# A modulation vector computed on VectorE in two batches instead of on GpSimd and ScalarE in one

## The chip, the cores and the metric

The kernel runs on one core of a Trainium2 chip. The metric is the device time of one execution in microseconds. Three executions of the kernel before took 1995.58, 1997.78 and 2001.44 us; the median is 1997.78 us.

## The reference, cut to what matters

Two transformer blocks are applied one after the other to 512 tokens of 1024 features, all in float32. Block 1 is a mixer (an mLSTM branch and a sparse attention branch, "NSA", joined and projected by `w_out`) followed by a norm. Block 2 has three sublayers: a SwiGLU feed-forward net (FFN1), a token mixer with a delta rule, and a second feed-forward net (FFN2). Before each sublayer the normed values are shifted and scaled, and each sublayer's result is gated, by vectors that depend on a second input `c` alone:

```python
mod = (jax.nn.silu(c) @ ada_w[l] + ada_b[l]).reshape(B, N_SUBLAYERS, 3, D_MODEL)
shift, scale, gate = mod[:, :, 0], mod[:, :, 1], mod[:, :, 2]
h = modulate(rms_norm(x, norm_g[l, 0]), shift[:, 0], scale[:, 0])
x = x + 0.5 * gate[:, 0, None, :] * swiglu(h, ffn1_w_in[l], ffn1_w_out[l])
```

`ada_w` is 1024 x 9216 (37.7 MB). Its product with one vector is the modulation: nine parts of 1024 values (shift, scale and gate of three sublayers), which the kernel holds as 72 columns of 128. The change is about where and when these 72 columns are computed. FFN1 needs columns 0 to 15 for its norm and 16 to 23 for its gate, the mixer needs 24 to 47, FFN2 needs 48 to 71. Nothing in block 1's values depends on them.

## The kernel before

**The large products.** A plan is a list of groups (`Group`); each group is a product of 512 tokens with up to 1024 x 128 (or x 256, 264, 288, 512) weights. `run` walks the plan. For each piece of 128 x 1024 weights it emits a load into one of three `wr` buffers (line 302), a split into two float32r parts, `wh` on ScalarE and `wl` as a difference on VectorE (two pieces ahead of the product that uses them), and 24 matrix products of 512 columns into a `pg` bank of PSUM (four banks). When a group is full, its bank is read by ScalarE or VectorE ("evacuated").

**The side work.** After each group and in its middle `run` calls `side_step`, which advances the generators in `self.side` (mLSTM, NSA, norms, delta rule) and in `self.bg`. A generator that waits for a flag yields "w".

**The order of the instructions.** The program is emitted in that order, but the framework reorders each engine's instructions by priority (what was emitted earlier goes first) and by its own estimate of when operands and buffers are free. An instruction that was emitted late but whose operands are ready early can therefore stand much earlier in its engine's queue. Each queue is fixed in the built program, and on the chip an engine goes through it strictly in order.

**The modulation before** (`ada`, line 629 on). A generator in `self.bg` starts once block 1's norm is done. It takes 144 half columns: a load of 128 x 512 weights (`adaw`, line 646) into a slot of the common pool, a product with silu(c) (tile `sc`) by GpSimd (`tt` with `eng=nc.gpsimd`, line 220), and a copy by ScalarE that sums each row into one value of `adap` (`accum_out`, line 217, which makes a second instruction on ScalarE, the read of the accumulator). Two loads are in flight. At the end 72 pairs are added and the scale, shift and gate tiles are made. `ada_done`, ahead of the projection by `w_out` (`w_o1`), drains `self.bg`.

**What else the names mean.** `pg` is a bank of a large product, `hh`/`hl` and `uh`/`ul` are split values, `wh`/`wl` split weights; `cx`, `ca`, `ct`, `mqk` are the steps of the convolution that follows the `w_q` and `w_k` groups (line 613 on: two ScalarE reads of the bank, three VectorE steps `ca`, a tanh `ct`, a product `mqk`); `mrow`, `gcol`, `mS` and `mE` belong to the mLSTM; `cs`, `csx`, `cpt`, `sS`, `smx`, `sP`, `src`, `sPT` to NSA (`sP` are the exponentials that GpSimd scales by `src`). `sd` and `su` are two 128 x 1024 tiles of a pool `solve` with one buffer each; the compression of NSA's keys uses them as `kk`, and block 2's delta rule uses them later.

Of the kernel before, what the change touches and what calls it, by code (L numbers as in the profile page):

```python
# [18 lines left out]
P = 128  # L19
# [9 lines left out]
GS = 2                  # heads whose triangles are solved together  # L29
SOLVE_STEP = 4          # columns of them between two products  # L30
SOLVE_DELAY = 7         # steps until the solved ones are back from memory
NV = 2                  # groups of values, of gates, that start before a norm
# [63 lines left out]
def prep(a):  # L96
    """Lays the inputs out for the loads: name -> array."""
# [60 lines left out]
class Group:  # L158
    """One group of a large product: pieces of weights, and what to do with them."""
# [9 lines left out]
class Call:  # L169
    """A place in the plan where something else is put into the program."""  # L170
# [6 lines left out]
class Builder:  # L177
# [56 lines left out]
    def trr(self, out, in_):  # L234
        """transpose of values that float32r holds"""
        return self.nc.tensor.transpose(out.bitcast(F32R), in_, self.identr)
# [9 lines left out]
    def pow(self, out, in_, n):  # L246
        """out = in ** -0.5"""
        self.nc.gpsimd.tensor_tensor(out, in_, self.mhalf[:, 0:n], OP.pow)
# [34 lines left out]
    def later(self, f, *a):  # L283
        """evacuate now, or when the norm that the values lack is there"""
        if self.hold is None:
            with self.tc.high_priority(offset=0):
                f(*a)
        else:
            self.hold.append((f, a))
# [6 lines left out]
    def load(self, upto):  # L296
        """starts the loads of the weights, up to a piece"""
# [8 lines left out]
    def part(self, upto):  # L306
        """splits weights into the two parts that the products take"""
# [15 lines left out]
    def run(self, plan, ahead_dma=3, ahead_split=2):  # L323
# [5 lines left out]
        for g in plan:  # L329
# [6 lines left out]
            for k0, n in g.pieces:  # L336
# [4 lines left out]
                if g.early:  # L341
                    # whole tiles of tokens, one after another: the first in banks of the side work
# [35 lines left out]
                elif g.halves:  # L378
                    if k0 == 0:
                        ps = [self.pg.tile([P, 512], F32, tag="g", name="pg") for _ in range(2)]  # L380
                    if g.mid and k0 + n == g.kts:
                        # the first half of the tokens is done before the second
# [66 lines left out]
    def copies(self):  # L449
        """of the constants, in other types"""  # L450
# [11 lines left out]
    def rows_to_bcast(self, cols4, name, inorder=False):  # L462
        """[128, 4] token columns -> a bank [128, 512] with every row the 512 values"""
# [7 lines left out]
    def colsum(self, sq, ps, c0):  # L471
        """sums over features of sq, as token columns ps[:, c0 + t]"""
# [15 lines left out]
    def rstd(self, ps, c0, name):  # L488
        """token columns: (sum / D + eps) ** -0.5"""
# [6 lines left out]
    def u_add(self, f, x, g, shift=None):  # L496
        """x * g, split, for the products that start before the norm is known; the shift beside it"""
# [8 lines left out]
    def unorm(self, pa, pb):  # L506
        """the product with the norm, and the column that the shift adds"""
# [7 lines left out]
    def norm(self, i):  # L515
        """the norm before a sublayer (i: of block 2, None: of block 1), beside its first products"""
# [64 lines left out]
    def start_norm(self, i):  # L581
        """in the plan, before the products on self.u"""
# [29 lines left out]
    def conv(self, ps, w, b, out):  # L612
        """2 * silu(conv of width 4 over the tokens + b), features on partitions"""
# [15 lines left out]
    def ada(self):  # L629
        nc = self.nc  # L630
        sc = []
        for h in range(2):
            s, th = self.slot("sc"), self.slot("scth")
            src = self.A["cvec"]
# [3 lines left out]
            sc.append(s)  # L638
        self.mod = self.const(72, "mod")
        part = self.const(144, "adap")  # L640
        ws = {}

        def load(i):
            if i < 144:
                ws[i] = self.slot("adaw")
                nc.sync.dma_start(ws[i], self.A["ada"][i // 2, :, i % 2 * 512:(i % 2 + 1) * 512])

        load(0)
        load(1)
        yield  # L650
        for i in range(144):
            load(i + 2)
            w = ws.pop(i)
            self.tt(w, w, sc[i % 2], OP.mult, eng=nc.gpsimd)
            yield
            self.act(w, w, AF.Copy, accum_out=part[:, i:i + 1])
        p2 = part.rearrange("p (f h) -> p f h", h=2)
        self.tt(self.mod, p2[:, :, 0], p2[:, :, 1], OP.add)
        self.stt(self.mod, self.mod, 0.5, self.c("ada_b"), OP.mult, OP.add)
        m = self.mod  # L660
        self.A_, self.S_, self.G_, self.SS = [], [], [], []
        for i in range(3):
            a = self.const(KT, f"A{i}")
# [3 lines left out]
            g = self.const(KT, f"G{i}")  # L667
            self.ts(g, m[:, i * 24 + 16:i * 24 + 24], 0.5 if i == 1 else 0.25, None, OP.mult)
            self.A_.append(a)
            sh = m[:, i * 24:i * 24 + 8]  # L670
            self.S_.append(sh)
            hi, lo = self.const(KT, f"SH{i}", F32R), self.const(KT, f"SL{i}", F32R)
            self.act(hi, sh)
            self.tt(lo, sh, hi.bitcast(F32), OP.subtract)
            self.SS.append((hi, lo))
            self.G_.append(g)
        self.flags.add("ada")

# [31 lines left out]
    def rope(self, dst, src, t, shape):  # L710
        """the first 16 of 64 of each head; dst, src: [128, a, b, 64]"""
# [13 lines left out]
    def block1(self):  # L725
# [209 lines left out]
        def ada_done():  # L935
            while self.bg:
                self.side_step()
            self.u, self.nacc, self.nacc2, self.x = [], None, None, {}

        plan.append(Call(ada_done))  # L940
# [20 lines left out]
    def compress(self):  # L961
        """keys and values of the 31 compressed blocks"""
        nc = self.nc
        self.vbd = []
        for j in range(2):
# [39 lines left out]
            if j == 0:  # L1005
                ps = self.bank("kcp")
                self.mm(ps[:, 0:64], w2, gl)
                # for two heads of a group at a time
# [23 lines left out]
    def nsa(self):  # L1032
# [6 lines left out]
        # keys, twice over the rows of a product: its high part, its low part  # L1039
# [923 lines left out]
```

## Time and profile before

| what | value |
|---|---|
| median of three executions | 1997.78 us |
| span of the profiled execution, first to last instruction | 1991.7 us |
| the profiled execution's own time | not listed apart from the three; its span is 6.1 us below their median |
| TensorE (PE) busy | 1922.1 us, 97% |
| VectorE (DVE) busy | 1142.3 us, 57% |
| ScalarE (ACT) busy | 872.8 us, 44% |
| GpSimd (POOL) busy | 509.6 us, 26% |
| mean granted TensorE clock | 0.987 |
| half columns of the modulation on GpSimd | 144, from 50.5 to 547.7 us of the span |

The stages follow one another in the span: mLSTM products until about 290 us (the four heads' `w_q`, `w_k`, `w_o`, `w_z`, `w_v`), NSA's inputs `w_c`, `w_kv`, `w_nq`, then `w_ba`, `w_nz`, `w_ga`, `w_gb` beside NSA's side work until about 560 us, `w_bb` and `w_out` until 677 us, FFN1's input products until 930 us, its output products until 1060 us, the mixer until about 1600 us, and FFN2. TensorE is the busiest engine in every one of them, so a microsecond is lost where TensorE waits or where its clock is granted at half; the profile gives both.

### The profile page before, as it was taken

To read this page: it belongs to the slowest core of one execution; us is meant where nothing else is said; L and a number is where in the kernel's file an instruction comes from. 1 tells how busy PE (TensorE), PEld (TensorE's weight loads), DVE (VectorE), ACT (ScalarE), POOL (GpSimd) and SP (SyncE) were. 2 spreads that over 40 slices of the span, in tenths; PEclk is the share of its full clock that TensorE was granted. 3 is DMA by queue.
4 is the path that set the end of the run, shared out by engine and by line. 5 is a ranking of instruction groups with operands and counts; after the bars stand their busy time and mean duration, and the time that the engine had idled before them with its cause. 6 is when DMAs were issued, how large, how long until landed. Compare 5 with 4: busy or idle time off the path is not lost. (4 is left out here: it accounts for less than half of the span.)

```text
span 1991.7 us, 27380 instructions
## 1 busy us (share of the span) xinstructions
PE 1922.1 (97%) x10296; PEld 1586.3 (80%) x10296; DVE 1142.3 (57%) x2059; ACT 872.8 (44%) x1856; POOL 509.6 (26%) x376
## 2 busy tenths in 40 slices
PE   8999999998999999999999999999999999999998
PEld 7779878786677888888888888867778897888887
DVE  7777674746655775333333769768755565333322
ACT  6565654656544443222222555645443343222221
POOL 2454443356621270000001433132210060000000
PEclk9999998999999999999999999999999999999999
DMA  5444445454311423333333233232332333333322
GB/s 182 137 147 143 159 136 174 148 187 160 109 43 37 154 78 102 94 93 92 103 109 109 80 94 88 85 100 67 82 105 85 122 101 96 95 95 95 95 88 72
DMA packets 100118, 216.21 MB, mean 109 GB/s; under 512 B 24721, under 2 KB 35857, under 8 KB 99985
## 3 DMA queue, kind: packets, MB, share of 16 engines
q1 hardware_dynamic: 95232, 208.27, 33.1%
q10 hardware_dynamic: 4752, 6.18, 1.0%
q8 instruction: 81, 1.33, 0.3%
q14 instruction: 53, 0.43, 0.1%
HBM read 206.55 MB, written 7.34 MB: 107 GB/s over the span
## 5 line engine op out<-in xcount | busy, mean ns | idle before, releaser
L217 ACT ACTIVATE wh<-wr 128x1024 fp32r<-128x1024 f32 (+4 forms) x311 | 315.2, 1014 | 643.3 <-issue 366.4
L220 DVE TENSOR_TENSOR wl<-wr,wh 128x1024 fp32r<-128x1024 f32 (+4 forms) x289 | 357.2, 1236 | 390.4 <-ACT wh L217 383.0
L229 PE MATMUL pg<-hh,wh 128*128 128x512 f32 x1240 | 501.2, 404 | 1.3 <-DVE un L220 1.3
L229 PE MATMUL pg<-hl,wh 128*128 128x512 f32 x1240 | 493.0, 398 | 0.9 <-DVE hl L226 0.9
L229 PE MATMUL pg<-hh,wl 128*128 128x512 f32 x1240 | 492.4, 397 | 0.0
L229 PEld LDWEIGHTS pg<-hh,wl 128*128 128x128 f32 x1240 | 234.5, 189 | 54.7 <-issue 0.2
L229 PEld LDWEIGHTS pg<-hh,wh 128*128 128x128 f32 x1240 | 235.4, 190 | 52.4 <-issue 2.1
L229 PEld LDWEIGHTS pg<-hl,wh 128*128 128x128 f32 x1240 | 235.1, 190 | 52.1 <-DVE hl L226 1.4
L220 POOL TENSOR_TENSOR adaw<-adaw,sc 128x512 f32<-128x512 f32 x144 | 216.4, 1523 | 228.5 <-DMA adaw<-in_ada 199.1
L220 POOL TENSOR_TENSOR nacc<-nacc,sq 128x512 f32<-128x512 f32 x34 | 47.6, 1406 | 786.4 <-ACT sq L217 786.3
L229 PE MATMUL pg<-wh,hh 128*128 128x256 f32 (+2 forms) x512 | 161.1, 315 | 11.2 <-ACT ca L217 8.8
L229 PE MATMUL pg<-wh,hl 128*128 128x256 f32 (+2 forms) x512 | 153.2, 302 | 1.0 <-DVE hl L220 0.7
L229 PE MATMUL pg<-wl,hh 128*128 128x256 f32 (+2 forms) x512 | 153.9, 301 | 0.0
L229 PE MATMUL pg<-fah,wh 128*128 128x512 f32 (+1 forms) x374 | 140.1, 382 | 0.0
L229 PE MATMUL pg<-fah,wl 128*128 128x512 f32 (+1 forms) x374 | 139.9, 381 | 0.0
L229 PE MATMUL pg<-fal,wh 128*128 128x512 f32 (+1 forms) x374 | 139.7, 380 | 0.0
L217 ACT ACTIVATE adaw<-adaw 128x512 f32<-128x512 f32 x144 | 90.9, 632 | 111.2 <-POOL adaw L220 109.1
L226 DVE SCALAR_TENSOR_TENSOR ca<-cx,cols,ca 128x511 f32<-128x511 f32 (+2 forms) x120 | 113.8, 948 | 24.3 <-ACT ca L217 22.3
L229 PEld LDWEIGHTS pg<-wh,hh 128*128 128x128 f32 x512 | 98.8, 193 | 21.2 <-ACT ca L217 9.7
L229 PEld LDWEIGHTS pg<-wl,hh 128*128 128x128 f32 x512 | 98.5, 192 | 4.6 <-issue 1.2
L229 PEld LDWEIGHTS pg<-wh,hl 128*128 128x128 f32 x512 | 97.9, 192 | 5.2 <-DVE hl L220 2.1
L220 POOL TENSOR_TENSOR wl<-wr,wh 128x1024 fp32r<-128x1024 f32 (+2 forms) x22 | 48.5, 2206 | 178.3 <-ACT wh L217 160.1
(431 smaller groups left out, 3217.8 us busy)
## 6 DMA issues: line engine op xcount, KB each, us to landing
adaw<-in_ada SPq DMA_DIRECT2D x144, 256.0 KB
wr<-in_f1i SPq DMA_DIRECT2D x44, 512.0 KB
wr<-in_f2i SPq DMA_DIRECT2D x44, 512.0 KB
wr<-in_m_qkv SPq DMA_DIRECT2D x24, 512.0 KB
wr<-in_w_o SPq DMA_DIRECT2D x16, 512.0 KB
wr<-in_f1o SPq DMA_DIRECT2D x16, 512.0 KB
wr<-in_m_g SPq DMA_DIRECT2D x16, 512.0 KB
wr<-in_f2o SPq DMA_DIRECT2D x16, 512.0 KB
```

The source lines that it names most:

```text
L217: return self.nc.scalar.activation(out, in_, f, bias=bias, scale=scale, **k)
L220: return (eng or self.nc.vector).tensor_tensor(out, a, b, op)
L226: return self.nc.vector.scalar_tensor_tensor(out, a, s, b, op0=op0, op1=op1, **k)
L229: return self.nc.tensor.matmul(out, lhsT, rhs, start=start, stop=stop, **k)
```

## The change

Columns are now taken whole: one load of 128 x 1024 weights into `sd` or `su` in turn (two buffers for all columns), and two fused VectorE instructions, each a product with 0.5 and with silu(c) that also sums its rows into one value of `adap`. GpSimd and ScalarE have no part in it any more. The generator makes columns 0 to 15, sets flag `ada0` (which `w_out` waits for in the plan), waits for flag `ffn1`, which is set after FFN1's first three pairs of groups, and then emits columns 16 to 39 and 40 to 71 with flags `ada1` and `ada2`. In FFN1 a product is written in place, which saves one slot a group. Comments and docstrings were removed too; that part of the diff is left out.

```diff
-        for i in range(144):
-            load(i + 2)
-            w = ws.pop(i)
-            self.tt(w, w, sc[i % 2], OP.mult, eng=nc.gpsimd)
+        def load(i):
+            ws[i] = self.sv.tile([P, D], F32, tag=("sd", "su")[i % 2], name="adaw")
+            nc.sync.dma_start(ws[i], self.A["ada"][i])
+
+        def columns(a, b, spread=1):
+            load(a)
+            load(a + 1)
             yield
-            self.act(w, w, AF.Copy, accum_out=part[:, i:i + 1])
-        p2 = part.rearrange("p (f h) -> p f h", h=2)
-        self.tt(self.mod, p2[:, :, 0], p2[:, :, 1], OP.add)
-        self.stt(self.mod, self.mod, 0.5, self.c("ada_b"), OP.mult, OP.add)
...
+            for i in range(a, b):
+                w = ws.pop(i)
+                for h in range(2):
+                    x = w[:, h * 512:h * 512 + 512]
+                    self.stt(x, x, 0.5, sc[h], OP.mult, OP.mult, accum_out=part[:, 2 * i + h:2 * i + h + 1])
+                x = None
+                w = None
+                if i + 2 < b:
+                    load(i + 2)
+                for _ in range(spread):
+                    yield
+            self.tt(self.mod[:, a:b], p2[:, a:b, 0], p2[:, a:b, 1], OP.add)
+            self.tt(self.mod[:, a:b], self.mod[:, a:b], self.c("ada_b", a, b), OP.add)
...
+        yield from columns(0, 16, 2)
+        sublayer(0)
+        self.flags.add("ada0")
+        yield from self.wait("ffn1")
+        yield from columns(16, 40)
+        gate(0)
+        sublayer(1)
+        self.flags.add("ada1")
+        yield from columns(40, 72)
...
+        self.flags.add("ada2")
...
-        def ada_done():
-            while self.bg:
-                self.side_step()
+        plan.append(self.until("ada0"))
...
-                s = self.slot("fa")
-                self.tt(s, th, ps, OP.mult)
+                self.tt(th, th, ps, OP.mult)
                 self.gp = None
-                self.act_[f] = self.split(s, "fa")
+                self.act_[f] = self.split(th, "fa")
...
+                if i == 0:
+                    plan.append(Call(lambda: self.flags.add("ffn1")))
```

What this does to the queues is seen at three places. First SP's queue, which issues the loads, from `w_nq` on. Before, half columns stand between the loads of the weights:

```order
L302 DMA wr<-in_w_nq 128x1024 x2
L646 DMA adaw<-in_ada 128x512 x4
L302 DMA wr<-in_w_nq 128x1024
L646 DMA adaw<-in_ada 128x512
L302 DMA wr<-in_w_nq 128x1024
L646 DMA adaw<-in_ada 128x512 x2
L302 DMA wr<-in_w_ba 128x1024 x2
L646 DMA adaw<-in_ada 128x512 x4
```

And now, from the same loads on, and at the end of this stage:

```order
L302 DMA wr<-in_w_nq 128x1024 x3
L649 DMA adaw<-in_ada 128x1024
L302 DMA wr<-in_w_nq 128x1024
L649 DMA adaw<-in_ada 128x1024
L302 DMA wr<-in_w_ba 128x1024
L649 DMA adaw<-in_ada 128x1024
...
L302 DMA wr<-in_w_gb 128x1024
L649 DMA adaw<-in_ada 128x1024 x4
L302 DMA wr<-in_w_gb 128x1024 x3
L302 DMA wr<-in_w_bb 128x512 x8
L302 DMA wr<-in_w_o 128x1024 x8
L302 DMA wr<-in_f1i 128x1024 x44
```

The second batch of 56 columns, which is emitted beside FFN1's input products (`f1i`), stands in the queues of block 1: it begins as soon as the compression has given back `sd` and `su`, and its last load stands ahead of the last three pieces of `w_gb`. Between `w_kv` and the first of these rows there is no column at all, since the first 16 columns stand further up.

Second, VectorE's queue near the start of block 1, at the first head's convolution and the mLSTM's row maxima `mrow`. Before:

```order
L226 SCALAR_TENSOR_TENSOR sc<-scth,sc 128x512
L220 TENSOR_TENSOR wl<-wr,wh 128x1024
L226 SCALAR_TENSOR_TENSOR sc<-scth,sc 128x512
L226 SCALAR_TENSOR_TENSOR ca<-cx,cols,ca 128x511
L226 SCALAR_TENSOR_TENSOR ca<-cx,cols,ca 128x510
L226 SCALAR_TENSOR_TENSOR ca<-cx,cols,ca 128x509
L226 SCALAR_TENSOR_TENSOR mqk<-ct,ca 128x512
L220 TENSOR_TENSOR wl<-wr,wh 128x1024
L1255 SCALAR_TENSOR_TENSOR mrow<-lfr,lir 4x512
```

Now:

```order
L226 SCALAR_TENSOR_TENSOR adaw,adap<-adaw,sc 128x512
L226 SCALAR_TENSOR_TENSOR sc<-scth,sc 128x512
L226 SCALAR_TENSOR_TENSOR ca<-cx,cols,ca 128x511
L226 SCALAR_TENSOR_TENSOR adaw,adap<-adaw,sc 128x512
L226 SCALAR_TENSOR_TENSOR ca<-cx,cols,ca 128x510
L226 SCALAR_TENSOR_TENSOR adaw,adap<-adaw,sc 128x512
L226 SCALAR_TENSOR_TENSOR ca<-cx,cols,ca 128x509
L220 TENSOR_TENSOR wl<-wr,wh 128x1024
L226 SCALAR_TENSOR_TENSOR mqk<-ct,ca 128x512
L226 SCALAR_TENSOR_TENSOR adaw,adap<-adaw,sc 128x512
L1279 SCALAR_TENSOR_TENSOR mrow<-lfr,lir 4x512
```

Five fused instructions of the modulation stand ahead of `mrow` that were not there (the first of them above this piece). All 32 of the first batch stand in the queue before the second head's convolutions.

Third, ScalarE's queue at the second head's convolutions. Before:

```order
L217 ACTIVATE cx<-pg 128x512
L217 ACTIVATE ca<-pg,cols 128x512
L217 ACTIVATE mh<-mH 128x256
L217 ACTIVATE adaw,adap<-adaw 128x512
L217 ACTIVATE ct<-ca 128x512
L217 ACTIVATE wh<-wr 128x1024
L217 ACTIVATE cx<-pg 128x512
L217 ACTIVATE ca<-pg,cols 128x512
L217 ACTIVATE adaw,adap<-adaw 128x512 x2
```

Now:

```order
L217 ACTIVATE cx<-pg 128x512
L217 ACTIVATE ca<-pg,cols 128x512
L217 ACTIVATE wh<-wr 128x1024
L217 ACTIVATE mh<-mH 128x256
L217 ACTIVATE SH_1808<-mod 128x8
L217 ACTIVATE ct<-ca 128x512
L217 ACTIVATE wh<-wr 128x1024
L217 ACTIVATE cx<-pg 128x512
L217 ACTIVATE ca<-pg,cols 128x512
```

The summing copies `adaw,adap` are gone from ScalarE; one small copy of the finished shift (`SH`) stands here instead.

## Rows read from the trace of the kernel before

**Rows 1.** The page: busy time of each engine and its share of the span.

```profile
PE 1922.1 (97%) x10296; PEld 1586.3 (80%) x10296; DVE 1142.3 (57%) x2059; ACT 872.8 (44%) x1856; POOL 509.6 (26%) x376
```

**Rows 2.** Busy time, granted clock and transfers by stretch; the first row names the columns.

```profile
core 0: us, PE busy (x) PEld busy (x) DVE busy (x) ACT busy (x) POOL busy (x), PEclk, DMA share, GB/s
45.00:111.00 66.00, 62.15 (x378) 53.09 (x377) 48.74 (x75) 41.51 (x95) 26.09 (x17) 0.97 0.44 146
111.00:331.00 220.00, 207.17 (x1285) 181.44 (x1284) 150.89 (x244) 124.23 (x296) 97.08 (x63) 0.98 0.46 150
331.00:560.00 229.00, 218.71 (x1080) 168.85 (x1079) 139.77 (x308) 132.50 (x324) 122.45 (x98) 0.96 0.46 150
705.00:930.00 225.00, 221.75 (x1092) 185.32 (x1091) 110.79 (x145) 68.83 (x90) 34.38 (x22) 0.99 0.30 91
1200.00:1450.00 250.00, 236.18 (x1519) 193.95 (x1518) 201.24 (x511) 135.38 (x386) 71.84 (x59) 0.98 0.30 85
850.00:900.00 50.00, 50.00 (x217) 40.37 (x216) 19.03 (x22) 14.05 (x18) 0.00 (x0) 1.00 0.31 95
```

**Rows 3.** TensorE's waits, 111 to 331 us: us in total, times, longest.

```profile
PE pg L229 <- ACT ca L217: 8.0, 3, 3.8
PE cps L229 <- DMA cw<-in_c_w: 1.8, 1, 1.8
PE pg L229 <- ACT tz L217: 1.6, 1, 1.6
PE mS L229 <- DVE mqk L226: 1.4, 1, 1.4
```

**Rows 4.** ScalarE in order of time, 126 to 137 us: start, duration, [idle before].

```profile
127.48 0.77 ACT L217 ACTIVATE ca<-pg,cols 128x512 f32<-128x512 f32 x1
131.00 0.63 ACT L217 ACTIVATE adaw<-adaw 128x512 f32<-128x512 f32 x1 [2.76 <-POOL adaw L220]
...
134.19 0.76 ACT L217 ACTIVATE ca<-pg,cols 128x512 f32<-128x512 f32 x1
```

**Rows 5.** The same stretches table over one half-clock stretch.

```profile
135.80:139.20 3.40, 3.40 (x18) 3.40 (x17) 3.33 (x4) 1.32 (x3) 1.15 (x2) 0.50 0.90 319
```

**Rows 6.** Instructions on tile `adaw`: duration in ns min/median/max, first and last start.

```profile
L220 POOL TENSOR_TENSOR adaw<-adaw,sc x144: 1257/1300/2398, 50.5 to 546.4; 128x512 f32<-128x512 f32 x144
L217 ACT ACTIVATE adaw<-adaw x144: 612/632/670, 52.1 to 547.7; 128x512 f32<-128x512 f32 x144
L217 ACT ACTIVATION_READ_ACCUMULATOR adaw<-adaw x144: 183/187/238, 52.6 to 548.2; 128x1 f32 x144
```

**Rows 7.** The page's costliest groups: ScalarE's sums, busy, mean, idle before.

```profile
L217 ACT ACTIVATE adaw<-adaw 128x512 f32<-128x512 f32 x144 | 90.9, 632 | 111.2 <-POOL adaw L220 109.1
```

**Rows 8.** TensorE's waits, 331 to 560 us.

```profile
PE cpt L232 <- DVE csx L226: 4.5, 2, 2.8
PE sPT L232 <- POOL sP L220: 2.6, 1, 2.6
PE vcp L229 <- issue: 2.2, 1, 2.2
```

**Rows 9.** Fused products on tiles `mqk` and `ma`, as in rows 6.

```profile
L226 DVE SCALAR_TENSOR_TENSOR mqk<-ct,ca x16: 683/693/1790, 56.5 to 282.0; 128x512 f32<-128x512 f32 x16
L226 DVE SCALAR_TENSOR_TENSOR ma<-tga,ma x8: 677/679/1780, 477.6 to 551.4; 128x512 f32<-128x512 f32 x8
```

**Rows 10.** VectorE's weight differences, 45:111, 331:560 and 760:950 us: busy, mean ns.

```profile
L220 DVE TENSOR_TENSOR wl<-wr,wh 128x1024 fp32r<-128x1024 f32 x9 | 12.7, 1406 | 5.5 <-ACT wh L217 5.5
...
L220 DVE TENSOR_TENSOR wl<-wr,wh 128x1024 fp32r<-128x1024 f32 x28 | 42.0, 1498 | 41.2 <-ACT wh L217 34.6 <-PE sPT L232 3.6 <-DMA adaw<-in_ada 3.0
...
L220 DVE TENSOR_TENSOR wl<-wr,wh 128x1024 fp32r<-128x1024 f32 x35 | 42.9, 1225 | 66.0 <-ACT wh L217 66.0
```

**Rows 11.** A load of two half columns, and the GpSimd product that waited for it.

```profile
371.55 0.91 SPq L646 DMA_DIRECT2D adaw<-in_ada  x2
...
375.48 2.54 POOL L220 TENSOR_TENSOR adaw<-adaw,sc 128x512 f32<-128x512 f32 x2 [7.57 <-DMA adaw<-in_ada]
```

More of the change, by code (lines that the diff above doesn't have):

```diff
@@ L631, in ada @@
         sc = []
+        src = self.A["cvec"]
         for h in range(2):
             s, th = self.slot("sc"), self.slot("scth")
-            src = self.A["cvec"]
             nc.sync.dma_start(s, bass.AP(tensor=src.tensor, offset=src.offset + h * 512, ap=[[0, P], [1, 512]]))
@@ L638, in ada, with sublayer @@
             sc.append(s)
+        s = th = None
         self.mod = self.const(72, "mod")
         part = self.const(144, "adap")
+        p2 = part.rearrange("p (f h) -> p f h", h=2)
         ws = {}
         def load(i):
[L644 to L650, printed above, removed]
-        for i in range(144):
-            load(i + 2)
-            w = ws.pop(i)
-            self.tt(w, w, sc[i % 2], OP.mult, eng=nc.gpsimd)
-            yield
-            self.act(w, w, AF.Copy, accum_out=part[:, i:i + 1])
-        p2 = part.rearrange("p (f h) -> p f h", h=2)
-        self.tt(self.mod, p2[:, :, 0], p2[:, :, 1], OP.add)
-        self.stt(self.mod, self.mod, 0.5, self.c("ada_b"), OP.mult, OP.add)
[L660 to L663, printed above, removed]
+            ws[i] = self.sv.tile([P, D], F32, tag=("sd", "su")[i % 2], name="adaw")
[3 more added lines that the diff above has]
+            load(a + 1)
+            yield
+            for i in range(a, b):
[11 more added lines that the diff above has]
+            self.tt(self.mod[:, a:b], self.mod[:, a:b], self.c("ada_b", a, b), OP.add)
+        def sublayer(i):
+            a, m = self.const(KT, f"A{i}"), self.mod
             self.stt(a, m[:, i * 24 + 8:i * 24 + 16], 1.0, self.c("norm_g2", i * 8, i * 8 + 8), OP.add, OP.mult)
@@ L666, in ada @@
                 self.tt(a, a, self.c("final_norm_g"), OP.mult)
-            g = self.const(KT, f"G{i}")
-            self.ts(g, m[:, i * 24 + 16:i * 24 + 24], 0.5 if i == 1 else 0.25, None, OP.mult)
-            self.A_.append(a)
             sh = m[:, i * 24:i * 24 + 8]
-            self.S_.append(sh)
             hi, lo = self.const(KT, f"SH{i}", F32R), self.const(KT, f"SL{i}", F32R)
@@ L674, in ada, with gate @@
             self.tt(lo, sh, hi.bitcast(F32), OP.subtract)
+            self.A_.append(a)
+            self.S_.append(sh)
             self.SS.append((hi, lo))
+        def gate(i):
+            g = self.const(KT, f"G{i}")
+            self.ts(g, self.mod[:, i * 24 + 16:i * 24 + 24], 0.5 if i == 1 else 0.25, None, OP.mult)
             self.G_.append(g)
-        self.flags.add("ada")
+        self.A_, self.S_, self.G_, self.SS = [], [], [], []
+        yield from columns(0, 16, 2)
[7 more added lines that the diff above has]
+        yield from columns(40, 72)
+        gate(1)
+        sublayer(2)
+        gate(2)
+        sc.clear()
+        self.flags.add("ada2")
     def rope_tables(self):
@@ L933, in block1, with out_begins @@
         plan.append(self.free("yb"))
-        def ada_done():
-            while self.bg:
-                self.side_step()
+        plan.append(self.until("ada0"))
+        def out_begins():
             self.u, self.nacc, self.nacc2, self.x = [], None, None, {}
-        plan.append(Call(ada_done))
+        plan.append(Call(out_begins))
         def pre_out(f):
@@ L1422, in ffn @@
                 plan.append(self.free("u", "rbc"))
+                if i == 0:
+                    plan.append(Call(lambda: self.flags.add("ffn1")))
+        if i == 0:
+            plan.append(self.until("ada1"))
         def half():
@@ L1609, in mixer @@
         us = lambda: self.u
+        plan.append(self.until("ada2"))
         plan.append(self.start_norm(1))
```

## The prediction

> **What bounds the kernel now.** I read the page's busy times first: TensorE is busy for 97% of the span [rows 1], so the other engines matter only where they make it wait. Next I cut the span into stretches [rows 2]. FFN1's input products (705 to 930 us) leave TensorE idle for 225 - 221.75 = 3.3 us, all near their start; the modulation, before, is worked on from 50.5 to 547.7 us [rows 6], and there the losses lie. A stretch loses its idle time and, where the clock is granted at half, (1 - PEclk) of its length:
>
> - stretch E, 45 to 111 us: 66 - 62.15 = 3.9 us idle, 0.03 x 66 = 2.0 us by the clock, 5.9 us together;
> - stretch L, 111 to 331 us: 12.8 us idle and 0.02 x 220 = 4.4 us, 17.2 us;
> - stretch B, 331 to 560 us: 10.3 us idle and 0.04 x 229 = 9.2 us, 19.5 us.
>
> That is 42.6 us, the most that a change to the modulation could give. The waits tell how. In L the longest are for ScalarE's reads `ca` of a product's bank, 8.0 us in three waits [rows 3]. In order of time one of them reads thus [rows 4]: after `ca` at 127.48 us the next on ScalarE is a sum of the modulation, which starts at 131.00 after 2.76 us of waiting for GpSimd's product; the next `ca` starts only at 134.19, and TensorE, which has no free bank, waits 3.8 us. [...] So a ScalarE that goes through its queue in order was held by GpSimd, 109.1 us in all [rows 7], and GpSimd by loads. In B the waits are for `csx` and for `sP` [rows 8], tiles that pass through VectorE, ScalarE and GpSimd between two TensorE steps.
>
> **What is removed.** 144 products on GpSimd of 1300 ns (median) and on ScalarE 144 sums of 632 ns with 144 accumulator reads of 187 ns [rows 6]: 144 x 0.819 = 118 us of ScalarE's work and its 109 us of waits. A second effect is on VectorE. The same fused product `mqk` takes 683 ns at best and 1790 at worst, `ma` 677 and 1780 [rows 9]; the weight difference takes 1225 ns on average where GpSimd is silent, 1406 in E and 1498 in B [rows 10]. I read this as the two engines being in each other's way. From the differences alone: nine `wl` in E give 9 x 0.18 = 1.6 us, 28 in B 28 x 0.27 = 7.6 us. These are about a fifth to a third of VectorE's time there, and the other two-operand instructions are stretched likewise; I estimate 7 us of relief in E and 20 us in B, with 2 and 8 us as low ends.
>
> **What is added.** 144 fused products on VectorE, each with a sum. No VectorE instruction that sums is in the trace. From below it costs what `ma` and `mqk` cost, 0.68 to 0.69 us; from above one accumulator read as long as ScalarE's 0.187 us more, 0.88 us, if it is paid on the engine at all, and twice the streaming part if both operands and the sum don't fit: 512 elements more take 1.225 - 0.69 = 0.53 us (a difference of 1024 against a fused product of 512, [rows 9, 10]), so 0.69 + 0.53 = 1.22 us. I take 0.80 us, near the plain instruction. [...]
>
> **Where it lies.** The second batch is not beside FFN1: the queues have its 56 columns among `w_nq` to `w_gb`, in stretch B, and the first 16 columns in E; L has none.
>
> *Stretch L* loses all of its modulation work. ScalarE is 124 of 220 us busy with it and VectorE 151, so without it neither is full. Of the waits for `ca`, `tz` and `mS` (11.0 us) and the clock's 4.4 us I take some four fifths, 12.5 us; the wait for `cw` (1.8 us) is a load and stays. Bounds: 0 and 17.2.
>
> *Stretch E* gets 32 fused products. VectorE: 48.7 - 7 + 32 x 0.80 = 67.3 us for a stretch of 66: full. Five of them stand ahead of `mrow`, for which TensorE waits in E, so that comes up to 5 x 0.8 = 4 us later, less what the `ca` and `sc` in front win. There are also two buffers only. A load of 256 KB landed 375.48 - 371.55 = 3.9 us after its issue [rows 11]; 319 GB/s at a busy share of 0.90 [rows 5] is 355 GB/s for all queues, so 256 KB more take 0.7 us, 4.7 us in all, and where three columns stand in a row VectorE waits about 3 us with its queue (evacuations and weight differences) behind it. I take 3 us lost on top of today's 5.9; bounds -3 and +15.
>
> *Stretch B* gets 112. VectorE: 139.8 - 20 + 112 x 0.80 = 209 us of 229, 91%. What an engine this full does to TensorE can be read from the mixer, where VectorE is 201 of 250 us busy, 80%: 13.8 us idle and 0.02 x 250 = 5.0 us by the clock [rows 2], 7.5% of the stretch, which is 17.2 us on 229. ScalarE and GpSimd no longer hold `csx` and `sP`; VectorE's fused products stand between the steps of the same chains instead. Two columns need one round of both buffers, 4.7 + 2 x 0.8 + 0.3 for the issue = 6.6 us; 28 rounds take 185 of 229 us. Where the queue pairs two columns with each piece of weights, a piece takes TensorE 24 x 0.23 = 5.5 us (217 products in 50 us of FFN1, the last of [rows 2]), less than a round, but it has NSA's products beside it and weights split two pieces ahead. The weights' loads stand behind those of the columns on SP, with the same two pieces of cover; once that is gone the excess of about 1 us a piece over 20 pieces would show. I take 17.5 us lost for today's 19.5: 2 us won. Bounds: 15 us won, 27 lost.
>
> *Nothing* for the product written in place in FFN1 (the same instruction on another tile, TensorE full there), for the modulation's 20 or so small column operations, or for the halved number of loads (the bytes are the same).
>
> Sum: -12.5 + 3 - 2 = -11.5 us on a span of 1991.7 us gives 1980.2. The median lies 6.1 us above that span, so I add 6.1: 1986 us.
>
> **The rivals.** *VectorE gives it back.* L wins 12.5 us, but a full VectorE, or one that waits for its two buffers, makes E and B lose 8 us each: 3.5 us more than now, 2001 us. For it: 67 us of work in 66, 209 in 229. Against: banks are read by ScalarE in `w_ba` to `w_gb`, and the mixer lives with 80%.
>
> *The summing product is slow (slower than before).* At 1.22 us B needs 139.8 - 20 + 112 x 1.22 = 256 us of VectorE in 229, E 41.7 + 32 x 1.22 = 81 in 66; less the 12.5 of L that is 27 + 15 - 12.5 = +29, 2027 us. It turns from a gain into a loss where (119.8 + 112c - 229) + (41.7 + 32c - 66) = 12.5, at c = 1.01 us. For it: no summing instruction is shown. Against: `mqk` and `ma`, with both operands in SBUF as float32, run at 0.68 to 0.69 us. [...]
>
> *Everything wins.* Without ScalarE and GpSimd in front of them the chains of B run free as well: 12.5 + 15 = 27.5 us, 1970 us. For it: all of B's named waits pass through engines that the modulation held. Against: VectorE at 91%.
>
> **How the numbers follow.** 0.3% is 6 us, about what a measurement of this kernel can tell from no change. The forecast (1978 to 1994) has 0.50, giving it back 0.24, slow sums 0.13, everything wins 0.13. Faster than 1991.8: 0.45 + 0.13 = 0.58. Within: 0.05 of the forecast and 0.15 of giving it back, 0.20. Slower than 2003.8: 0.09 + 0.13 = 0.22. The range reaches from 1970 to 2015; beyond it lie most of the slow sums and a part of the last rival.
>
> **What would show it.** Between 111 and about 320 us no wait of TensorE for `ca` and no half-clock stretch; ScalarE without `adaw`; the fused product at 0.7 to 0.9 us; VectorE over 90% busy up to about 115 us and near 90% from `w_nq` to `w_gb`, with no `adaw` in FFN1; TensorE's losses in B about as large as before, now for VectorE. Wrong would be: waits of `wl` or of a bank behind `adaw` that add up to more than L gives, or a fused product over 1.0 us.

## The result, and the profile after

The changed kernel takes 1972.26 us (median; 1968.86 to 1974.32) beside 1999.54 us for the kernel before (four executions now): a ratio of 0.986, 95% interval 0.9842 to 0.9877. That is 27.3 us won where 11.5 were forecast. The sign was right; the gain was more than twice the forecast.

The page's busy line answers to [rows 1]. VectorE has the 144 fused products and is busy only 18 us longer; GpSimd has lost 211 us.

```profile
PE 1915.8 (97%) x10296; PEld 1582.0 (80%) x10296; DVE 1160.0 (59%) x2351; ACT 782.6 (40%) x1568; POOL 298.3 (15%) x232
```

The stretches of [rows 2] in the changed kernel (columns as there):

```profile
45.00:111.00 66.00, 64.40 (x395) 54.81 (x396) 56.95 (x150) 32.15 (x64) 0.00 (x0) 1.00 0.64 199
111.00:331.00 220.00, 218.43 (x1362) 192.72 (x1361) 129.45 (x269) 92.70 (x186) 4.90 (x6) 0.98 0.32 96
331.00:560.00 229.00, 223.86 (x1137) 169.39 (x1136) 185.02 (x546) 97.08 (x212) 37.16 (x36) 1.00 0.61 189
705.00:930.00 225.00, 224.29 (x1012) 182.88 (x1013) 102.47 (x130) 67.63 (x87) 13.30 (x9) 1.00 0.31 92
```

Idle TensorE is down to 1.6, 1.6 and 5.1 us in E, L and B, and no clock is lost in E and B. VectorE, which was to be full, is busy for 57 of 66 and 185 of 229 us. What the modulation has of that is shown by the same table for tile `adaw` alone:

```profile
45.00:111.00 66.00, 21.45 (x64) 1.00 0.64 199
...
331.00:560.00 229.00, 77.99 (x218) 1.00 0.61 189
```

So VectorE's other work takes 57.0 - 21.5 = 35.5 us in E and 185.0 - 78.0 = 107.0 in B, where it took 48.7 and 139.8 before [rows 2]: 13 and 33 us less. (The windows hold a little other work than before, since the kernel runs ahead.)

TensorE's waits in E for `mrow`, first before, then in the changed kernel (us, times, longest):

```profile
PE gcol L229 <- DVE mrow L1255: 2.5, 1, 2.5
```

```profile
PE gcol L229 <- DVE mrow L1279: 1.2, 1, 1.2
```

And in the changed kernel from 111 to 331 us (one row) and from 331 to 560, which answer to [rows 3, 8]: the waits for `ca`, `tz` and `mS` are gone, those for `csx` and `sP` are left.

```profile
PE cps L229 <- DMA cw<-in_c_w: 1.5, 1, 1.5
```

```profile
PE cpt L232 <- DVE csx L226: 3.2, 2, 2.6
PE sPT L232 <- POOL sP L220: 2.0, 1, 2.0
```

One sign that the prediction gave did not come: L keeps a stretch at half the clock, 6.8 us at its end (first row). The version without any modulation work (e6_nothing, below) has one too at that place (second row), so this one is not the modulation's.

```profile
312.80:319.60 6.80, 6.80 (x25) 6.03 (x24) 1.23 (x7) 0.58 (x2) 0.00 (x0) 0.50 0.65 207
```

```profile
310.20:320.40 10.20, 10.20 (x40) 9.14 (x39) 1.57 (x7) 0.57 (x2) 0.00 (x0) 0.50 0.56 166
```

The fused product by tile [rows 6], with the time for which VectorE sat idle until a load of it had landed (us, times), and after it the plain fused products `mqk` and `ma` [rows 9], none of which is stretched any more:

```profile
L226 DVE SCALAR_TENSOR_TENSOR adaw<-adaw,sc x144: 643/684/1518, 51.0 to 527.0; 128x512 f32<-128x512 f32 x144
L226 DVE DVE_READ_ACCUMULATOR adaw<-adaw,sc x144: 71/81/86, 51.6 to 527.6; 128x1 f32 x144
...
  DMA adaw<-in_ada: 26.0, 23
```

```profile
L226 DVE SCALAR_TENSOR_TENSOR mqk<-ct,ca x16: 683/692/693, 58.3 to 262.3; 128x512 f32<-128x512 f32 x16
```

```profile
L226 DVE SCALAR_TENSOR_TENSOR ma<-tga,ma x8: 675/680/683, 451.3 to 523.2; 128x512 f32<-128x512 f32 x8
```

The summing form costs what the plain one costs: 0.684 us in the median beside 0.692 for `mqk` and 0.680 for `ma`. It makes two instructions, 144 of each. In order of time VectorE shows that the second, the read of the accumulator (0.08 us), starts in the same 10 ns as the next instruction and adds nothing there (start, duration).

```profile
54.62 0.68 DVE L226 SCALAR_TENSOR_TENSOR adaw<-adaw,sc 128x512 f32<-128x512 f32 x1
55.23 0.08 DVE L226 DVE_READ_ACCUMULATOR adaw<-adaw,sc 128x1 f32 x1
55.23 0.75 DVE L226 SCALAR_TENSOR_TENSOR ca<-cx,cols,ca 128x510 f32<-128x510 f32 x1
55.89 0.68 DVE L226 SCALAR_TENSOR_TENSOR adaw<-adaw,sc 128x512 f32<-128x512 f32 x1
```

To see where the time went I paired TensorE's 8250 products of the large groups in each trace, in order, with those of the kernel before, and took the difference of their starts (us; negative is ahead; the column's time is that of the kernel before, and its product the last that starts there ahead of it):

| kernel | 45 | 111 | 331 | 560 | 1350 | last |
|---|---|---|---|---|---|---|
| the change | 1.5 | -2.9 | -19.1 | -28.1 | -30.0 | -24.5 |
| e1_engines | -0.6 | -5.5 | -20.6 | -38.2 | -39.9 | -34.3 |
| e2_place | 0.1 | 8.1 | -5.4 | 35.5 | 35.9 | 36.5 |
| e3_no_sums | 0.0 | 0.3 | -8.2 | -8.4 | -9.3 | -3.3 |
| e4_no_products | 0.1 | -4.8 | -21.3 | -37.0 | -39.4 | -33.8 |
| e8_swapped | 0.4 | 1.2 | -5.3 | -11.9 | -10.5 | -5.0 |
| e10_one_operand | 0.2 | -2.9 | -19.3 | -29.1 | -29.9 | -23.9 |
| e11_half_width | -0.1 | -2.8 | -18.4 | -31.6 | -31.1 | -30.9 |
| e5_in_ffn1 | 0.3 | -2.3 | -18.5 | -38.3 | -35.0 | -28.8 |
| e9_slots | 0.1 | -3.7 | -20.2 | -36.9 | -38.2 | -35.9 |
| e6_nothing | 0.6 | -4.4 | -20.9 | -36.1 | -32.3 | -25.6 |

The change wins 4.4 us in E (1.5 + 2.9), 16.2 in L and 9.0 in B. (At 331 us the kernel before is in a half-clock stretch; one product later the rows of that column differ by up to 2.9 us, so the border between L and B is good to some 3 us.) Some 5 us are lost again in the mixer, far from any modulation: between 1300 and 1450 us the changed kernel has 6.8 and 10.2 us (the row below) at half the clock, and the kernel before twice 3.4, and half of the difference is (17.0 - 6.8) / 2 = 5.1 us. Such stretches fall differently in each kernel, so the columns up to 560 are the cleaner measure.

```profile
1405.00:1415.20 10.20, 10.20 (x50) 8.06 (x48) 4.39 (x11) 5.20 (x14) 0.72 (x1) 0.50 0.16 57
```

### The profile page after: what moved, and what is told of

Its sections match the earlier page's. It is cut to its first block, busy times and chain, and to the rows that moved or that the text cites. A ratio compares the mean times of both kernels' runs of the same rounds, so it can differ in the third digit from the quotient of the medians.

```text
span 1967.1 us, 27022 instructions
## 1 busy us (share of the span) xinstructions
PE 1915.8 (97%) x10296; PEld 1582.0 (80%) x10296; DVE 1160.0 (59%) x2351; ACT 782.6 (40%) x1568; POOL 298.3 (15%) x232
## 5 line engine op out<-in xcount | busy, mean ns | idle before, releaser
L220 DVE TENSOR_TENSOR wl<-wr,wh 128x1024 fp32r<-128x1024 f32 (+4 forms) x289 | 343.5, 1189 | 362.2 <-ACT wh L217 359.7
L226 DVE SCALAR_TENSOR_TENSOR adaw<-adaw,sc 128x512 f32<-128x512 f32 x144 | 100.7, 717 | 26.0 <-DMA adaw<-in_ada 26.0
L226 DVE SCALAR_TENSOR_TENSOR ca<-cx,cols,ca 128x511 f32<-128x511 f32 (+2 forms) x120 | 99.3, 827 | 24.4 <-ACT ca L217 22.5
L220 DVE TENSOR_TENSOR fth<-fth,pg 128x512 f32<-128x512 f32 x38 | 26.1, 688 | 104.0 <-PE pg L229 104.0
L220 POOL TENSOR_TENSOR sP<-sP,src 128x512 f32<-128x512 f32 (+1 forms) x44 | 46.6, 1060 | 241.0 <-DVE src L220 225.2
```

The lines of the kernel that those rows point to most:

```text
L220: return (eng or self.nc.vector).tensor_tensor(out, a, b, op)
L226: return self.nc.vector.scalar_tensor_tensor(out, a, s, b, op0=op0, op1=op1, **k)
```

## The experiments

**Engines or place.** e1_engines is the kernel before with only the engines changed: half columns, slots and places as they were.

```diff
-            self.tt(w, w, sc[i % 2], OP.mult, eng=nc.gpsimd)
+            self.stt(w, w, 0.5, sc[i % 2], OP.mult, OP.mult, accum_out=part[:, i:i + 1])
...
             yield
-            self.act(w, w, AF.Copy, accum_out=part[:, i:i + 1])
...
```

> The kernel before with the engines changed alone: its 144 half columns stay where they are, in slots, two loads in flight, but product and sum are one fused VectorE instruction; GpSimd and ScalarE do nothing for the modulation. If the gain of 27 us comes from freeing ScalarE and GpSimd (theory: engines), nearly all of it shows: 1970 to 1980 us, no wait for ca between 111 and 331 us. If it comes from where the columns lie, the middle of block 1 being empty of them (theory: place), little shows: 1992 to 2000 us.

Measured: 1959.33 us, ratio 0.981 (0.9787 to 0.9833). This is faster than even the range of the theory "engines"; the engines alone win more than the whole change. L is not emptied here; VectorE works more in it than before, and TensorE is as free as in the changed kernel (one wait for `ca` is left, 0.6 us):

```profile
111.00:331.00 220.00, 217.61 (x1369) 191.56 (x1368) 161.89 (x389) 92.67 (x188) 3.02 (x3) 1.00 0.50 165
331.00:560.00 229.00, 227.41 (x1186) 172.67 (x1185) 159.20 (x458) 98.07 (x220) 40.00 (x41) 1.00 0.41 135
```

e2_place is the other half: the changed kernel with each product on GpSimd and each sum on ScalarE again.

```diff
-                    self.stt(x, x, 0.5, sc[h], OP.mult, OP.mult, accum_out=part[:, 2 * i + h:2 * i + h + 1])
+                    self.tt(x, x, sc[h], OP.mult, eng=nc.gpsimd)
+                    self.act(x, x, AF.Copy, scale=0.5, accum_out=part[:, 2 * i + h:2 * i + h + 1])
```

> The changed kernel with the engines changed back: whole columns, 16 early and 56 from w_nq on, in two buffers, but the product on GpSimd and the sum on ScalarE (two halves a column). Theory engines: no gain in the stretches that hold columns, and the 56 columns held together make ScalarE wait more there: 1985 to 2005 us. Theory place: the 16 us of the empty stretch and most of the rest stay: 1972 to 1980 us.

Measured: 2031.26 us, ratio 1.0175 (1.0153 to 1.0196). The new places with the old engines lose 34 us, which is slower than both theories had it. B alone loses 41 (from -5.4 to 35.5), where 112 GpSimd products now stand; TensorE's longest waits there and the fused product `ma` are these.

```profile
PE cpt L232 <- DVE csx L226: 13.2, 3, 5.2
PE sPT L232 <- POOL sP L220: 7.7, 3, 6.0
```

```profile
L226 DVE SCALAR_TENSOR_TENSOR ma<-tga,ma x8: 1524/1774/1818, 499.1 to 584.6; 128x512 f32<-128x512 f32 x8
```

**Which of the two engines.** e3_no_sums is the kernel before without ScalarE's 144 sums (the modulation stays at its bias); e4_no_products is the one without GpSimd's 144 products (ScalarE sums the raw weights).

```diff
-            self.act(w, w, AF.Copy, accum_out=part[:, i:i + 1])       # e3_no_sums
...
-            self.tt(w, w, sc[i % 2], OP.mult, eng=nc.gpsimd)          # e4_no_products
```

> The kernel before without ScalarE's 144 sums (the modulation is left at its bias): GpSimd's products and all loads stay. If ScalarE, held in its queue by GpSimd's products, is the cause (theory: held queue), about 25 us are won: 1972 to 1980 us, although VectorE's two-operand instructions stay stretched to over 1.2 us beside GpSimd. If the stretched VectorE is the cause (theory: shared access), 0 to 8 us: 1991 to 2000 us.

> The kernel before without GpSimd's 144 products (ScalarE sums the weights as loaded, so the modulation is wrong): ScalarE keeps 118 us of sums and now waits for the loads themselves. Theory shared access: VectorE runs unstretched, most of the gain: 1974 to 1982 us. Theory held queue: ScalarE is still held, by loads now, but no longer behind a product that takes its turn after them: 1985 to 1997 us.

Measured: e3_no_sums 1984.13 us, ratio 0.9937 (0.9916 to 0.9958); e4_no_products 1959.88 us, ratio 0.981 (0.9793 to 0.9828). The first lies between the ranges of its two theories, so neither effect is the whole; the second is faster than both of its ranges. With all of ScalarE's sums still there, ScalarE busy for 130 us of L (row below), the kernel without GpSimd's products is as fast as e1_engines. So ScalarE's 118 us of work cost nothing by themselves that shows here; GpSimd's products did. But this takes away both of the things that they can do: hold ScalarE, which waits 109.1 us for them [rows 7], and slow VectorE, whose `ma` takes up to 1.78 us beside them [rows 9].

```profile
111.00:331.00 220.00, 218.39 (x1364) 192.97 (x1363) 125.01 (x249) 130.46 (x314) 3.02 (x3) 0.98 0.51 165
```

**Held, or slowed.** e8_swapped keeps every product and every sum, but ScalarE sums first and GpSimd multiplies afterwards, so that only the next user of the buffer waits for GpSimd: mostly the next load, and two VectorE steps of NSA that take such a slot, for 3.0 us together.

```diff
-            self.tt(w, w, sc[i % 2], OP.mult, eng=nc.gpsimd)
             yield
             self.act(w, w, AF.Copy, accum_out=part[:, i:i + 1])
+            self.tt(w, w, sc[i % 2], OP.mult, eng=nc.gpsimd)
```

> The kernel before, but ScalarE sums the raw weights first and GpSimd multiplies the same tile afterwards, so that nothing but the buffer's next load waits for GpSimd's product; GpSimd's 144 products (1.30 us) and ScalarE's 144 sums stay. The modulation's values are not the reference's. Kernel before about 1997 us; without the products (e4_no_products) 1960. Theory 'VectorE is slowed beside GpSimd': what the products cost is the stretching of VectorE's two-operand instructions, which stays here: 1985 to 1997 us, fused products mqk and ma still up to 1.5 to 1.8 us, VectorE about 150 us busy in 111 to 331. Rival 'the held queue': ScalarE stood behind GpSimd's product, which it does no longer: 1960 to 1968 us, no wait of TensorE for ca between 111 and 331 us, although mqk and ma stay stretched.

Measured: 1986.61 us, ratio 0.9919 (0.9893 to 0.9946), within the first theory's bounds, near their fast end. In ratios, of the 1.9% that e4_no_products wins, 0.8% (16 us) was the hold and 1.1% (22 us) is the presence of GpSimd's products, for which almost nothing waits. e3_no_sums, which ends the hold in another way, wins 0.6%, the same within the intervals. The 1.1% is the cleaner number: in the traces of e8_swapped and e4_no_products VectorE, ScalarE and SP go through the same instructions in the same order (but for one transfer that ScalarE issues two places earlier), while from the kernel before to e8_swapped some of VectorE's and ScalarE's instructions change places too.

The path is seen in one place. VectorE's three `ca` steps of a convolution take 3.29 us in e8_swapped (first row below: start and duration) and 2.32 us in e4_no_products (second row). The three rows after them are what ScalarE does next in e8_swapped:

```profile
128.42 3.29 DVE L226 SCALAR_TENSOR_TENSOR ca<-cx,cols,ca 128x511 f32<-128x511 f32 x3 [0.46 <-ACT ca L217]
```

```profile
124.89 2.32 DVE L226 SCALAR_TENSOR_TENSOR ca<-cx,cols,ca 128x511 f32<-128x511 f32 x3 [0.46 <-ACT ca L217]
```

```profile
131.80 0.63 ACT L217 ACTIVATE ct<-ca 128x512 f32<-128x512 f32 x1 [0.45 <-DVE ca L226]
132.34 0.58 ACT L217 ACTIVATE cx<-pg 128x512 f32<-128x512 f32 x1
132.81 0.77 ACT L217 ACTIVATE ca<-pg,cols 128x512 f32<-128x512 f32 x1
```

ScalarE's tanh `ct` waits for that chain, and the next bank's two reads, `cx` and `ca`, stand behind `ct` in its queue. TensorE's longest waits in L thus still are for `ca` and for VectorE's `mqk` in e8_swapped, though no sum of the modulation waits for GpSimd; in e4_no_products both are gone. In e8_swapped:

```profile
PE pg L229 <- ACT ca L217: 4.2, 3, 1.7
PE mS L229 <- DVE mqk L226: 3.1, 1, 3.1
```

**How much GpSimd, and of which kind.** Two versions of e8_swapped with the same order on every engine (but for that transfer): e11_half_width multiplies 256 of the 512 columns, e10_one_operand multiplies all by a constant.

```diff
-            self.tt(w, w, sc[i % 2], OP.mult, eng=nc.gpsimd)
...
+            self.tt(w[:, 0:256], w[:, 0:256], sc[i % 2][:, 0:256], OP.mult, eng=nc.gpsimd)   # e11_half_width
+            self.ts(w, w, 0.5, None, OP.mult, eng=nc.gpsimd)                                 # e10_one_operand
```

> As e8_swapped, every engine's queue the same, but GpSimd multiplies only the first 256 of a tile's 512 columns. The modulation's values are not the reference's (they are not in e8_swapped either). e8_swapped 1987 us, without any product (e4_no_products) 1960. Theory 'GpSimd's streaming time beside VectorE is the price': half of the 27 us goes, 1970 to 1977 us; the share of two-operand VectorE instructions that run at 1.5 us or more falls by about half. Rival 'a fixed price for each product, by its queue or its semaphores': 1982 to 1988 us.

> As e8_swapped, every engine's queue the same, but GpSimd's product with silu(c) is a product with the constant 0.5: one streamed operand instead of two, on the same 128x512 tile. The modulation's values are not the reference's. e8_swapped 1987 us, without any product 1960. Theory 'any GpSimd pass over SBUF is in VectorE's way': as long as its instructions take on GpSimd (1.3 to 1.65 us), so 1980 to 1995 us, with mqk and ma up to 1.3 us or more. Rival 'only GpSimd instructions with two streamed operands are': 1958 to 1968 us, mqk and ma at 0.68 to 0.70 us.

Measured: e11_half_width 1965.80 us, ratio 0.9841 (0.9811 to 0.9871); e10_one_operand 1969.16 us, ratio 0.9855 (0.983 to 0.9879). Tile `adaw` on GpSimd and the fused product `ma`, first two rows with half the width, then two with one operand:

```profile
L220 POOL TENSOR_TENSOR adaw<-adaw,sc x144: 723/742/2636, 52.0 to 514.6; 128x256 f32<-128x256 f32 x144
```

```profile
L226 DVE SCALAR_TENSOR_TENSOR ma<-tga,ma x8: 679/688/1226, 450.3 to 519.4; 128x512 f32<-128x512 f32 x8
```

```profile
L223 POOL TENSOR_SCALAR adaw<-adaw x144: 1483/1492/3228, 52.5 to 518.6; 128x512 f32<-128x512 f32 x144
```

```profile
L226 DVE SCALAR_TENSOR_TENSOR ma<-tga,ma x8: 682/888/1530, 448.7 to 521.9; 128x512 f32<-128x512 f32 x8
```

I summed the durations of VectorE's 190 or so instructions on the tiles `wl`, `ca`, `mqk`, `mEl`, `tz`, `to` and `ma` between 45 and 560 us: 203 us before and in e8_swapped, 175 with half the width, 171 with one operand, 160 in e4_no_products. Half of GpSimd's streaming leaves a third of the stretch (15 of 43 us) and about a quarter of the time lost (0.0031 of 0.0109 in the ratios; 6 of 27 us in the medians). The intervals of e11_half_width and e4_no_products overlap, so the quarter is rough, but there is no fixed price for a product, and the time came out below what even the first theory gave (1970 to 1977 us). With one operand GpSimd's instructions take longer than in e8_swapped and stretch VectorE by 11 us instead of 43; the time lost is between a third and two fifths (0.0045 of 0.0109; at 560 us 7.9 of 25.1). So the rival is nearer, though the time is 1 us above its range and `ma` still reaches 1.53 us: mostly two streamed operands are in VectorE's way, but not they alone.

This run also bounds two other readings of what GpSimd's presence costs: that GpSimd's own steps, `sP` above all, stand behind the products in its queue, and that buffers come back late. Both would cost no less with passes of 1.49 us than with products of 1.30, so the two together are at most 7.9 of the 25.1 us. Of these 7.9 us 5.9 lie in B (9.8 won there, 15.7 in e4_no_products), where TensorE's longest wait in e10_one_operand is for `sP`; whether that wait or the rest of VectorE's stretch costs them is not shown.

```profile
PE sPT L232 <- POOL sP L220: 3.6, 1, 3.6
```

**Where the second batch stands.** e5_in_ffn1 makes it wait for FFN1, by writing two values of FFN1's last input tile into each of `sd` and `su` first; e9_slots loads half columns into slots of the pool, which has the same effect on the place.

```diff
+        for t, kt in (("sd", 0), ("su", 1)):
+            gate_t = self.sv.tile([P, D], F32, tag=t, name="adag")
+            nc.vector.tensor_copy(gate_t[:, 0:2], self.h[KT - 1][kt][:, 0:2].bitcast(F32))   # e5_in_ffn1
...
-            ws[i] = self.sv.tile([P, D], F32, tag=("sd", "su")[i % 2], name="adaw")
-            nc.sync.dma_start(ws[i], self.A["ada"][i])
+            ws[i] = [self.slot("adaw"), self.slot("adaw")]                                   # e9_slots
+            for h in range(2):
+                nc.sync.dma_start(ws[i][h], self.A["ada"][i, :, h * 512:(h + 1) * 512])
...
```

> The changed kernel, but the second batch's two tiles are first written from FFN1's last normed tile, so that its 56 columns lie beside FFN1's input products (SP's queue has all 56 loads among f1i). Changed kernel 1972 us, kernel e1_engines (same fused products at the old places) 1959. Theory 'the burst of 112 fused products in the gates' stretch is what the placement costs': 331 to 560 us wins most of what e1_engines wins over the change there, some 7 us, and FFN1, where VectorE goes from 111 to 111 + 112 x 0.77 = 197 us busy of 225 and nothing else hangs on it but the weight splits and its own product, loses at most 2: 1964 to 1968 us. Rival 'a full VectorE costs wherever it is': FFN1 loses 7 us or more by waits for wl or for banks behind adaw, which gives the gain back: 1970 to 1978 us. Third: the difference to e1_engines lies outside the gates' stretch (start, 312 to 320 us): 1972 less whatever B wins, under 3 us.

> As the changed kernel, but a column is loaded as two half columns of 256 KB into slots of the common pool (up to four in flight) instead of one of 512 KB into one of two buffers; by this its second batch stands beside FFN1's input products too. Against e5_in_ffn1, which has the same place: theory 'two large buffers don't matter': within 4 us of e5_in_ffn1. Rival 'VectorE waits for its two buffers with its queue behind it': 5 us or more faster than e5_in_ffn1, with shorter idle of VectorE for the load of adaw than the change's 26 us in all.

Measured: e5_in_ffn1 1966.48 us, in the range of its first theory, ratio 0.9825 (0.9808 to 0.9842); e9_slots 1961.53 us, ratio 0.98 (0.978 to 0.9821). Both reach 560 us 9 to 10 us ahead of the change, and FFN1 bears 112 fused products at no cost to TensorE (e9_slots, B and FFN1):

```profile
331.00:560.00 229.00, 229.00 (x1195) 174.38 (x1194) 118.66 (x330) 99.69 (x218) 35.13 (x38) 1.00 0.21 65
705.00:930.00 225.00, 225.00 (x994) 183.56 (x993) 169.44 (x357) 68.29 (x88) 4.31 (x3) 1.00 0.67 223
```

In FFN1 VectorE waits for the loads 29.6 us with two large buffers and 3.0 us with slots (first row e5_in_ffn1, second e9_slots), and it doesn't matter: at 1200 us the two stand at -37.6 and -38.2. So the rival of the two buffers falls in its reason, although the medians lie 5 us apart as it had it. These 5 us come later, in the mixer, where e5_in_ffn1 has a half-clock stretch like the changed kernel's (the third row) that e9_slots lacks.

```profile
L226 DVE SCALAR_TENSOR_TENSOR adaw<-adaw,sc 128x512 f32<-128x512 f32 x112 | 73.2, 689 | 29.8 <-DMA adaw<-in_ada 29.6
```

```profile
L226 DVE SCALAR_TENSOR_TENSOR adaw<-adaw,sc 128x512 f32<-128x512 f32 x112 | 73.6, 687 | 3.2 <-DMA adaw<-in_ada 3.0
```

```profile
1399.80:1410.00 10.20, 10.20 (x50) 8.06 (x49) 4.29 (x11) 5.36 (x14) 0.47 (x1) 0.50 0.21 53
```

**The floor.** e6_nothing is the changed kernel without the modulation's loads and products.

```diff
-            load(a)
-            load(a + 1)
...
-                w = ws.pop(i)
-                for h in range(2):
-                    x = w[:, h * 512:h * 512 + 512]
-                    self.stt(x, x, 0.5, sc[h], OP.mult, OP.mult, accum_out=part[:, 2 * i + h:2 * i + h + 1])
...
-                if i + 2 < b:
-                    load(i + 2)
```

> The changed kernel without the modulation's loads and products (its value is left at the bias): the floor under every version. Theory 'all but 3 to 5 us of what the modulation costs is gone in e1_engines and e4_no_products' (1959 and 1960): 1953 to 1957 us. Rival 'fused products on VectorE or the 37.7 MB of loads still cost as much again': 1940 to 1948 us. By the prediction's own account the three stretches lost 42.6 us, so 1998 - 42.6 = 1955 if every loss of theirs were the modulation's.

Measured: 1962.41 us, ratio 0.9799 (0.9777 to 0.9821), slower than both ranges. Up to 560 us it is 36.1 us ahead, no more than e1_engines, e4_no_products and e9_slots (36.9 to 38.2): they leave nothing of the modulation's cost that this can measure. Behind that it loses 10.5 us again, without any modulation: from 560 to 1450 us it is at half the clock for 30.6 us (the longest stretch in the row), the kernel before for 13.6.

```profile
1402.50:1412.70 10.20, 10.20 (x51) 8.06 (x50) 4.14 (x11) 5.45 (x14) 0.40 (x1) 0.50 0.21 53
```

Both e1_engines and e9_slots beat the changed kernel: their intervals (up to 0.9833 and 0.9821) lie below the change's (from 0.9842). The change itself pays some 10 us for its burst in B, the 112 products that stand there close together.

## Why the prediction was wrong, step by step

**The step that failed.** The sum had 3 us lost in E, 12.5 won in L and 2 won in B; the starts give 4.4, 16.2 and 9.0 us won (and 1.5 lost ahead of E). So E and B hold 14.4 us of the miss and L 3.7. What failed is the pricing of VectorE in E and B: the relief from GpSimd was sized too small and counted as room for the new products alone, and a busy share was taken for a price. In its place the runs show that GpSimd's products cost TensorE time in every stretch, though almost nothing waits for them: between e8_swapped and e4_no_products lie 5.7 us in E, 10.0 in L and 9.1 in B. By e10_one_operand, which keeps 7.9 of the 25.1 us with passes of 1.49 us, most of this goes through VectorE's stretched chains.

**The cause of L's losses.** I read one wait of ScalarE for GpSimd [rows 4, 7] as the cause of L's 17.2 us, and so expected the win because L is emptied. The size was near (12.5 forecast, 16.2 measured), by luck, since the reason was not: e1_engines leaves L full and wins 15.1 there (-5.5 to -20.6). Undoing the hold alone (e8_swapped) wins 6.5 of it, taking the products away 16.5 (e4_no_products). The larger part, 10.0 us, is that GpSimd stretches VectorE's chains, on which ScalarE's queue also waits. The very wait of [rows 4] shows both in the kernel before: `ct`, behind the held sum, began at 132.58 us (second row), but the `ca` steps for which it also waits ended only at 128.28 + 3.23 = 131.51 us (first row), so an earlier sum could have let `ct` begin 1.1 us earlier at most.

```profile
128.28 3.23 DVE L226 SCALAR_TENSOR_TENSOR ca<-cx,cols,ca 128x511 f32<-128x511 f32 x3 [0.18 <-ACT ca L217]
```

```profile
132.58 0.61 ACT L217 ACTIVATE ct<-ca 128x512 f32<-128x512 f32 x1
```

**The relief of VectorE.** The prediction had the right rows for it [rows 9, 10], but estimated 7 us in E and 20 in B from the mean of `wl`, in proportion the least stretched of the groups; the accounts above give 13 and 33. It also used the relief only to make room for the new products. That a shorter VectorE step is itself time on TensorE's path (25 us up to 560 us: -11.9 in e8_swapped against -37.0 in e4_no_products) stood nowhere in the sum. With the fused product at 0.69 us instead of 0.80, VectorE was 57 of 66 us busy and not 67, and 185 of 229 and not 209.

**The price of a full VectorE.** E was to lose 3 us and won 4.4: `mrow`, said to come up to 4 us later, made TensorE wait 1.2 us instead of 2.5. B was to lose 17.5 us, by the mixer's rate at a VectorE 80% busy; with 81% it loses 5.1 and wins 9.0 where 2 were forecast. A busy share prices nothing by itself: FFN1 in e9_slots has VectorE 75% busy (169 of 225) and TensorE idle for 0.0 us, where, by the plan, only the weight splits and its own products hang on it. That B still pays for the burst was right, some 9 us (9.0 won against 17.6 in e1_engines), and as the prediction had it the waits that stay are `csx` and `sP`.

**The place.** That the 56 columns stand in B and not in FFN1 was right (last fused product at 527.0 us), and e2_place shows how much the places matter with the old engines.

**The rivals.** The slow summing product falls: 0.684 us at 128x512 in float32, the plain form's time, where this rival had 1.22. No run shows the second 0.53 us of streaming that it added. "VectorE gives it back" falls as well. "Everything wins" (27.5 us) came out in size, partly by luck: it had 15 us from B, where 9.0 were won, and nothing from E. In its reason it was half right: the chains of B run freer, but not free.

**How far the stretch goes.** VectorE's `ma` goes from 677 to at most 1780 ns beside products of 1.30 us [rows 9], and from 679 to 1226 beside products of 0.74 (e11_half_width). These worst stretches, 1.10 and 0.55 us, are each shorter than the median GpSimd product beside them. So the stretch shrinks with the product, but its length alone does not set it: beside the one-operand passes of 1.49 us `ma` is stretched by 0.85 us at most, and the 48 `ca` steps, which take 0.75 us in the median, reach 1.10 at most. By what mechanism GpSimd stretches VectorE is not shown.

## What to carry to other kernels

Where the same VectorE instruction shows 0.68 us at best and 1.78 at worst, look at what GpSimd streams at that moment, and price the stretch on the chain that TensorE waits for, not only as room on VectorE. A product moved from GpSimd to VectorE can cost less than nothing (e1_engines takes 0.981 of the time); spread evenly, or put where nothing but buffers hang on VectorE, 144 of them cost nothing here that could be measured, while 112 in one burst between the steps of a dependent chain took back some 10 of 38 us. A busy share says little about the price (at 75% in e9_slots' FFN1 TensorE idled 0.0 us, at 81% the burst in B cost some 9); what is queued behind it does.

## What the runs showed of the hardware

- Two-operand GpSimd products of 128x512 (1.30 us) and two-operand VectorE instructions stretch each other: `ma` up to 1.78 us from 0.68 [rows 9], and in the kernel before two GpSimd products in a row took 2.51 us at 144.5 us, where VectorE stood idle, and 3.77 us at 133.0 us, beside VectorE's `wl`, `mqk` and `ca`. With half the columns in each GpSimd product 15 of the 43 us of stretch stay.
- A one-operand pass of GpSimd over the same tile takes longer (1.49 us against 1.30) and disturbs VectorE about a quarter as much (11 us of stretch against 43). Why is not settled by these runs.
- A VectorE fused product that sums its rows costs 0.68 us at 128x512 in float32 (144 in the changed kernel), as without the sum; its read of the accumulator lasts 0.08 us beside the next instruction.
